# New prices for transfers and strided copies in a kernel that orders itself by a timing model

## The chip, the cores and the metric

The kernel runs on one core of a Trainium2 chip. The metric is the device time of one execution in microseconds; smaller is better. Three runs of the kernel before gave a median of 2499.2 us.

## The reference

A bidirectional encoder trunk of two layers over 272 tokens (16 meta tokens and 256 of the sequence), width 2048, in float32. Each layer has a mixer and a channel mixer:

```python
hn = rms_norm(h, mix_norm[layer])
c_q, c_kv, k_rope, u = split(hn @ w_in[layer])
att = mla_attention(c_q, c_kv, k_rope, ...)        # 8 heads, softmax over all 272 tokens
ssm = s5_mixer(u, ...)                             # complex diagonal scan, forward and backward, 64 groups
h = h + concat(rms_norm(att), rms_norm(ssm)) @ w_out[layer]
hn = rms_norm(h, ffn_norm[layer])
h = h + swiglu(hn, ...)                            # layer 0: dense, hidden width 5632
h = h + moe_swiglu(hn, ...)                        # layer 1: top 2 of 8 experts, hidden width 1408
```

At the end comes a last `rms_norm`, and the 16 meta tokens are dropped.

## The kernel before

**Stages.** In time order: mixer of layer 0 (to about 350 us with the first half of its output product), dense feed-forward, mixer of layer 1, experts. The weights come from DRAM in blocks of 512 KB through a ring of five `raw` buffers. In layer 0 the first 40 blocks are used as they are; after them ACT makes a rounded copy `wh` and DVE the rest `wl`, and each step of a product is three matmuls (`XH` by `wh`, `XL` by `wh`, `XH` by `wl`).

**The state-space part.** The columns u of the input product come first, in eight tiles. Each is scaled by DVE and stored to DRAM (`put_u`, L1433, into `uscr`); a pair of tiles is read back in another layout by two transfers (`load_u`, L959). `ssm_x` (L1037) multiplies four such groups by the tiles V, writes the products to PSUM, and copies them from there into the array X with strided access: on ACT in layer 0, on ACT and DVE in layer 1. In layer 0 the V tiles are made during this time from two transfers each (`pscr` and `ssm_bT`) by four DVE operations (`v_load`, `v_make`, L967 to L989); for layer 1 they are made during the dense part and stored. `ssm_scan` (L1083) then runs 66 steps of four DVE operations over X. After the attention `ssm_h` (L1101) copies pieces of X into the ring `rh`, and `ssm_y` (L1277) multiplies them, adds the Toeplitz part (made by `w_all`, L1125, and held in DRAM), copies the result into the ring `ry`, transposes it and applies GELU with a strided write. The first half of the output product, `w_out` (L1607), runs beside it: 16 column tiles of 8 steps.

**The order of the work.** Every engine runs its instructions in the order in which the program emits them. That order is found while the program is built: the parts above are generators, and `Sched.run` (L486) steps a main one (the products) and a list of side ones. A generator yields a condition or a time. A time is due when the modelled clock of PE has reached it (`ready`, L462); a name stands for "DVE's modelled clock is less than so far ahead of PE's". Where nothing is due, the modelled clock of PE is moved on by 100 ns.

**The model.** `Model` (L245) keeps a clock for each engine and, for each piece of memory, when it was last written and read. Costs of one instruction come from `pe_cost`, `dve_cost` (L426) and `act_cost` (L432); to the end of each the entry of its engine in `OUT` (L248) is added before its result counts as there. `Model.dma` (L348) takes 500 ns for an issue (600 on the Pool queue), 650 ns to the start, one nanosecond for 90 elements, and `OUT["DMA"]` to the landing. `rdy` (L634) asks the model when memory is ready and adds 200 ns; the generators that follow a transfer yield that time: X after `load_u`, the V products after `v_load`, the Toeplitz part after its loads, `ssm_y` after its loads, the transposes of the experts' tokens after the gather (`fetch`, L1952, and `feeder`, L2017). None of these numbers is in the program that runs: there the semaphores hold each instruction until its data are there.

**Memory.** `Arena` (L70) gives out pieces of one large tile, from the low end unless `top` is asked for. `room` asks whether pieces would fit; several generators yield until they do.

Of the kernel before, what the change touches and what calls it, by code (L numbers as in the profile page):

```python
# [24 lines left out]
NC = 68  # L25
TC = 4
# [43 lines left out]
class Arena:  # L70


    def __init__(self, t, n):
        self.t, self.n, self.live = t, n, []
        self.peak = 0
# [52 lines left out]


class Ring:  # L130
    def __init__(self, arena, n, shape, p=128):
        self.h = [arena.get(shape, p) for _ in range(n)]
        self.i = 0

    def next(self):
# [109 lines left out]
class Model:  # L245


    OUT = {"PE": 197.0, "DVE": 127.0, "ACT": 152.0, "DMA": 960.0}  # L248

    def __init__(self):  # L250
        self.t = {"PE": 0.0, "DVE": 0.0, "ACT": 0.0, "DGE": 0.0, "DMA": 0.0}
# [84 lines left out]
    def mark(self, eng, e, ins, outs):  # L336
        e += self.OUT[eng]
        for ap in ins:
            n, u = self.where(ap)
            if u is not None:  # L340
                r = self.mem[n][1]
                r[u] = np.maximum(r[u], e)
        for ap in outs:
            n, u = self.where(ap)
            if u is not None:
                self.mem[n][0][u] = e

    def dma(self, q, out, *ins):  # L348
        t = max(self.q.get(q, 0.0), self.ready(*ins))
        n, u = self.where(out)  # L350
        if u is not None:
            t = max(t, self.mem[n][0][u].max(), self.mem[n][1][u].max())
        t = max(t, self.t["DGE"]) if q != "pool" else t
        e = t + (500.0 if q != "pool" else 600.0)
        self.q[q] = e
        if q != "pool":
            self.t["DGE"] = e
        d = max(self.t["DMA"], e + 650.0) + size_all(out) / 90.0
        self.t["DMA"] = d
        self.mark("DMA", d, ins, [out])  # L360
        if self.log is not None:
            self.log.append(("DMA", d - size_all(out) / 90.0, d, "dma"))
        return d + 960.0


def size_all(ap):
    n = 1
    for x in ap.shape:
        n *= x
    return n  # L370


def size(ap):
    n = 1
    for x in ap.shape[1:]:
        n *= x
    return n
# [35 lines left out]
def psum(ap):  # L413
    return "PSUM" in str(ap.space)
# [10 lines left out]

def dve_cost(name, a, k):  # L426
    n = size(a[0]) if name != "tensor_reduce" else size(a[1])
    f = 65.0 + (63.0 if any(psum(x) for x in a) else 0.0)
    return f + n * {"reciprocal": 6.4, "memset": 0.3, "tensor_scalar": 0.6}.get(name, 1.05)


def act_cost(name, a, k):  # L432
    return (52.0 if psum(a[1]) else 93.0) + (93.0 if "accum_out" in k else 0.0) + 0.84 * size(a[0])


class Proxy:
    def __init__(self, nc, sched):
        self._nc = nc
        m = sched.m
        self.vector = Eng(nc.vector, m, "DVE", dve_cost)  # L440
        self.scalar = Eng(nc.scalar, m, "ACT", act_cost)
        self.tensor = Eng(nc.tensor, m, "PE", pe_cost)
        self.sync = Eng(nc.sync, m, "SP", None)
        self.gpsimd = Eng(nc.gpsimd, m, "pool", None)
# [87 lines left out]
class Kern:  # L532
# [568 lines left out]
    def ssm_h(self, l, F):  # L1101

        nc, st = self.nc, self.st
        yield self.has("scan", l)
        yield self.has("att", l)
        yield lambda: F.room(2 * 4 * 2 * NC)
        X = st["X"]
        rh = st["rh"] = Ring(F, 2, [4, 2, NC])
        st["hq"], st["hn"], n = [], 0, 0
        for t in rh.h:  # L1110
            nc.vector.memset(t.ap, 0.0)
        for T in TORD:
            for a in (0, 4):
                yield lambda: n - st["hn"] < 2
                t = rh.next()
                yield self.s.m.clear(t)
                g = 8 * T + a
                nc.scalar.activation(t[0:64, :, :, 1:NC],
                                     X[0:64, :, :, g:g + 4].rearrange("p s r g -> p g r s"), AF.Copy)
                nc.vector.tensor_copy(t[64:128, :, :, 0:NC - 1],  # L1120
                                      X[64:128, ::-1, :, g:g + 4].rearrange("p s r g -> p g r s"))
                st["hq"].append((t, self.rdy(t)))
                n += 1
# [153 lines left out]
    def ssm_y(self, l, F):  # L1277

        nc, st = self.nc, self.st
        q0 = NMETA if l else 0  # L1280
        N, k0 = L - q0, q0 // TC
        yield self.has("scan", l)
        yield lambda: "rh" in st and self.R is not None and F.room(8 * N, 512, 512) and self.R.room(8 * N, 8 * N)
        R = self.R
        g_ = st["g"] = F.get([8, N], top=True)
        gh, gl = st["gh"], st["gl"] = R.get([8, N]), R.get([8, N])
        ry = Ring(F, 2, [TC, 8, 16], NC)
        idn = self.cst[:NC, CI:CI + NC]

        def turn(T, y, t):  # L1290
            yield t
            bank = yield from self.grab()
            ps = bank[:, :L].rearrange("p (t k) -> p t k", t=TC)
            for j in range(TC):
                nc.tensor.transpose(ps[:, j], y[:, j].rearrange("p g c -> p (g c)"), idn)
            nc.scalar.activation(g_[:, T].rearrange("p (k t) -> p t k", t=TC), ps[:, :, k0:], AF.Gelu_apprx_tanh)
            self.drop(bank)
            nc.scalar.activation(gh[:, T], g_[:, T], AF.Copy)
            yield self.rdy(gh[:, T])
            nc.vector.tensor_tensor(gl[:, T], g_[:, T], gh[:, T].bitcast(F32), op=OP.subtract)  # L1300
            st["nT"] += 1

        st["nT"] = 0
        for i, T in enumerate(TORD):
            yield lambda: i in st["wq"]
            w, m, u, t = st["wq"].pop(i)
            yield t
            yield lambda: i - st["nT"] < 2
            y = ry.next()
            bank = yield from self.grab()  # L1310
            ps = bank[:NC].rearrange("p (g t c) -> p g t c", g=8, t=TC)
            for a in (0, 4):
                yield lambda: len(st["hq"]) > 0
                H, t = st["hq"].pop(0)
                yield t
                for g in range(4):
                    b = (a + g) // GW[l], (a + g) % GW[l]
                    for r in range(2):
                        nc.tensor.matmul(ps[:, a + g], H[:, g, r], w[:, b[0], r, :, b[1]], start=(r == 0), stop=False)
                    nc.tensor.matmul(ps[:, a + g], u[:, a + g, T // 4],  # L1320
                                     m[:, a + g].rearrange("p (t c) -> p t c", t=TC), start=False, stop=True)
                    if g % 2:
                        yield None
                st["hn"] += 1
            st["yn"] = i + 1
            nc.scalar.activation(y.rearrange("p t g c -> p g t c"), ps, AF.Copy)
            self.drop(bank)
            self.s.add(turn(T, y, self.rdy(y)))
        yield lambda: st["nT"] == 8
        for r in (ry, st["rh"], st["U"], st["X"]) + st["rw"]:  # L1330
            r.free()
        self.flags.add(("Y", l))
# [1058 lines left out]
```

## Time and profile before

| | |
|---|---|
| median of three runs | 2499.2 us |
| lowest and highest | 2496.71 and 2500.32 us |
| the profiled execution's own time | 2494.38 us |
| its span, first to last instruction | 2492.5 us |
| its mean granted PE clock | 0.985 |
| busy: PE, DVE, ACT, Pool | 97%, 77%, 55%, 6% |

The profile is of one execution, shorter than the median; sums made from its rows stand against its own time. Busy time of PE is modelled at its ends, so a high share does not say that every matmul ran at full rate; the idle time in front of an instruction and the granted clock of a window say where time was lost. Nearly all operations are recorded at L408, the line of the wrapper that feeds the model, and all ordinary DMA issues at L390; so groups are told apart by the names of what they write and read. `fa` and `ra` are the arenas, `bank` is PSUM. A matmul on plain float32 data shows as two records.

### The profile page before, as it was taken

What the parts mean: (1) busy time and instruction counts of PE and PEld (TensorE: products, weight loads), DVE (VectorE), ACT (ScalarE), POOL (GpSimd) and SP (SyncE); (2) the same over time, 40 slices, a digit from 0 to 9 for tenths busy, and PEclk for the clock granted to TensorE, in tenths of its full rate; (3) what the DMA queues carried; (4) which work ended last, traced back from release to release, by engine and by line L of the source; (5) the groups of instructions that cost most, each with busy time, mean ns of one, the idle gap of its engine ahead of it and who ended that gap; (6) DMA issues with size and microseconds to landing.
All of it is one profiled execution on the core that took longest, in us unless ns stands there. A gap on an engine that the chain in (4) does not pass through costs nothing. (4 is left out here: it accounts for less than half of the span.)

```text
span 2492.5 us, 42294 instructions
## 1 busy us (share of the span) xinstructions
PE 2427.1 (97%) x15930; PEld 2187.0 (88%) x15930; DVE 1920.4 (77%) x3282; ACT 1375.0 (55%) x1876; POOL 152.2 (6%) x262
## 2 busy tenths in 40 slices
PE   8899999999999999999999899999999999999997
PEld 6676699999999999999999759987888888888886
DVE  8788657787766666555666987668999999999997
ACT  4324566443333333334455456546777877877775
POOL 3400110011100000000011001000000000000000
PEclk9999899999999999999999989999999999999998
DMA  7842554568755555555566316657999999999995
GB/s 258 230 149 86 141 157 151 167 215 269 261 187 194 188 191 190 172 177 170 178 205 195 127 44 204 236 201 271 387 355 350 385 341 371 365 330 372 360 336 198
DMA packets 192919, 583.47 MB, mean 234 GB/s; under 512 B 36225, under 2 KB 48897, under 8 KB 191553
## 3 DMA queue, kind: packets, MB, share of 16 engines
q1 hardware_dynamic: 174802, 520.42, 60.0%
q0 software_dynamic: 17040, 57.97, 7.7%
q8 instruction: 127, 2.08, 0.3%
q10 hardware_dynamic: 864, 2.28, 0.3%
q14 instruction: 86, 0.70, 0.1%
HBM read 560.14 MB, written 22.54 MB: 234 GB/s over the span
## 5 line engine op out<-in xcount | busy, mean ns | idle before, releaser
L408 DVE TENSOR_TENSOR wl<-raw,wh 128x1024 fp32r<-128x1024 f32 (+1 forms) x559 | 667.6, 1202 | 194.2 <-ACT wh L408 188.4
L408 ACT ACTIVATE wh<-raw 128x1024 fp32r<-128x1024 f32 (+1 forms) x559 | 579.8, 1040 | 318.9 <-PE bank L408 231.4
L408 PE MATMUL bank<-XH,wh 128*128 128x272 f32 (+1 forms) x2160 | 636.8, 295 | 0.8 <-ACT tmpr L408 0.5
L408 PE MATMUL bank<-XH,wl 128*128 128x272 f32 (+1 forms) x2160 | 623.0, 288 | 3.1 <-DVE wl L408 3.1
L408 PE MATMUL bank<-XL,wh 128*128 128x272 f32 (+1 forms) x2160 | 620.8, 287 | 1.6 <-DVE XL L408 1.3
L408 PEld LDWEIGHTS bank<-XH,wh 128*128 128x128 f32 x2160 | 407.6, 189 | 5.1 <-ACT tmpr L408 0.7
L408 PEld LDWEIGHTS bank<-XH,wl 128*128 128x128 f32 x2160 | 407.1, 188 | 4.5 <-DVE wl L408 4.5
L408 PEld LDWEIGHTS bank<-XL,wh 128*128 128x128 f32 x2160 | 407.9, 189 | 2.6 <-DVE XL L408 2.2
L408 PE MATMUL bank<-ra,wh 128*128 128x272 f32 (+1 forms) x1792 | 341.1, 290 | 1.8 <-ACT wh L408 1.8
L408 PEld LDWEIGHTS bank<-ra,wh 128*128 128x128 f32 x1792 | 280.7, 188 | 6.5 <-issue 2.4
L408 PE MATMUL bank<-fa 128*68 128x64 f32 (+11 forms) x1892 | 263.5, 279 | 21.9 <-DMA fa<-uscr 10.2
L408 PEld LDWEIGHTS bank<-fa 128*68 128x68 f32 (+6 forms) x1892 | 196.1, 161 | 83.8 <-issue 50.4
L408 DVE TENSOR_TENSOR fa<-fa 128x128 f32<-128x128 f32 (+9 forms) x687 | 236.2, 353 | 43.0 <-ACT fa L408 16.9
L408 PE MATMUL bank<-ra,wl 128*128 128x272 f32 (+1 forms) x896 | 256.6, 286 | 0.8 <-DVE wl L408 0.8
L408 PE MATMUL bank<-wh,XH 128*128 128x512 f32 (+1 forms) x584 | 222.6, 381 | 0.7 <-ACT fa L408 0.4
L408 ACT ACTIVATE fa<-bank 64x268 f32<-64x268 f32 (+9 forms) x281 | 138.6, 500 | 150.4 <-PE bank L408 133.2
L408 PE MATMUL bank<-wh,XL 128*128 128x512 f32 (+1 forms) x584 | 220.1, 377 | 0.0
L408 PE MATMUL bank<-wl,XH 128*128 128x512 f32 (+1 forms) x584 | 219.0, 375 | 0.0
L408 PE MATMUL bank<-wh,ra 128*128 128x512 f32 x552 | 185.7, 393 | 2.0 <-ACT fa L408 2.0
L408 PE MATMUL bank<-fa,raw 128*128 128x272 f32 x608 | 162.4, 405 | 7.2 <-DMA raw<-w_mix 6.4
L408 PEld LDWEIGHTS bank<-ra,wl 128*128 128x128 f32 x896 | 168.6, 188 | 1.0 <-DVE wl L408 1.0
L408 DVE TENSOR_TENSOR wl<-h,wh 128x1024 fp32r<-128x1024 f32 (+1 forms) x137 | 157.0, 1156 | 9.9 <-ACT wh L408 7.4
(127 smaller groups left out, 3232.6 us busy)
## 6 DMA issues: line engine op xcount, KB each, us to landing
raw<-w_dense SPq DMA_DIRECT2D x264, 512.0 KB, 3.4
raw<-w_mix SPq DMA_DIRECT2D x150, 512.0 KB, 3.4
raw<-w_moe_g SPq DMA_DIRECT2D x106, 512.0 KB, 5.5
h<-w_moe_g SPq DMA_DIRECT2D x80, 512.0 KB, 5.8
raw<-w_moe_d SPq DMA_DIRECT2D x73, 512.0 KB, 6.7
h<-w_moe_d SPq DMA_DIRECT2D x59, 512.0 KB, 6.6
raw<-w_moe_t SPq DMA_DIRECT2D x51, 384.0 KB, 4.0
h<-w_moe_t SPq DMA_DIRECT2D x44, 384.0 KB, 4.1
```

What stands on the lines that cost most here:

```text
L408: return f(*a, **k)
```

## The change

The entry of `OUT` for transfers goes from 960 to 2260 ns, and so does the same number in what `Model.dma` returns. A new test `apart` finds operands of three or more dimensions whose last one is not contiguous. ACT copies with such an operand, and DVE copies from PSUM into such an operand, are priced 80 ns plus 2.05 ns an element. The rings `rh` and `ry` are taken from the upper end of their arena; `Ring` has a new argument for that. No instruction is added or taken out; their order and the addresses of the two rings, and of what is placed after them, can differ.

```diff
--- before.py
+++ after.py
@@ -128,8 +128,8 @@
 
 
 class Ring:
-    def __init__(self, arena, n, shape, p=128):
-        self.h = [arena.get(shape, p) for _ in range(n)]
+    def __init__(self, arena, n, shape, p=128, top=False):
+        self.h = [arena.get(shape, p, **({"top": True} if top else {})) for _ in range(n)]
         self.i = 0
 
     def next(self):
@@ -245,7 +245,7 @@
 class Model:
 
 
-    OUT = {"PE": 197.0, "DVE": 127.0, "ACT": 152.0, "DMA": 960.0}
+    OUT = {"PE": 197.0, "DVE": 127.0, "ACT": 152.0, "DMA": 2260.0}
 
     def __init__(self):
         self.t = {"PE": 0.0, "DVE": 0.0, "ACT": 0.0, "DGE": 0.0, "DMA": 0.0}
@@ -360,7 +360,7 @@
         self.mark("DMA", d, ins, [out])
         if self.log is not None:
             self.log.append(("DMA", d - size_all(out) / 90.0, d, "dma"))
-        return d + 960.0
+        return d + 2260.0
 
 
 def size_all(ap):
@@ -425,11 +425,20 @@
 
 def dve_cost(name, a, k):
     n = size(a[0]) if name != "tensor_reduce" else size(a[1])
+    if name == "tensor_copy" and psum(a[1]) and apart(a[0]):
+        return 80.0 + 2.05 * n
     f = 65.0 + (63.0 if any(psum(x) for x in a) else 0.0)
     return f + n * {"reciprocal": 6.4, "memset": 0.3, "tensor_scalar": 0.6}.get(name, 1.05)
 
 
+def apart(ap):
+
+    return ap.ap[-1][0] != 1 and len(ap.shape) > 2
+
+
 def act_cost(name, a, k):
+    if apart(a[0]) or apart(a[1]):
+        return 80.0 + 2.05 * size(a[0])
     return (52.0 if psum(a[1]) else 93.0) + (93.0 if "accum_out" in k else 0.0) + 0.84 * size(a[0])
 
 
@@ -1105,7 +1114,7 @@
         yield self.has("att", l)
         yield lambda: F.room(2 * 4 * 2 * NC)
         X = st["X"]
-        rh = st["rh"] = Ring(F, 2, [4, 2, NC])
+        rh = st["rh"] = Ring(F, 2, [4, 2, NC], top=True)
         st["hq"], st["hn"], n = [], 0, 0
         for t in rh.h:
             nc.vector.memset(t.ap, 0.0)
@@ -1284,7 +1293,7 @@
         R = self.R
         g_ = st["g"] = F.get([8, N], top=True)
         gh, gl = st["gh"], st["gl"] = R.get([8, N]), R.get([8, N])
-        ry = Ring(F, 2, [TC, 8, 16], NC)
+        ry = Ring(F, 2, [TC, 8, 16], NC, top=True)
         idn = self.cst[:NC, CI:CI + NC]
 
         def turn(T, y, t):
```

## Rows read from the trace of the kernel before

**Rows 1.** The page's head: span; busy time, share of span, instructions of PE.

```profile
span 2492.5 us, 42294 instructions
...
PE 2427.1 (97%) x15930; PEld 2187.0 (88%) x15930; DVE 1920.4 (77%) x3282; ACT 1375.0 (55%) x1876; POOL 152.2 (6%) x262
```

**Rows 2.** Windows by stage: busy us (instructions) of PE, PEld, DVE, ACT, POOL; granted clock, DMA.

```profile
350.00:1300.00 950.00, 947.24 (x7492) 935.92 (x7491) 635.06 (x973) 394.88 (x506) 42.95 (x80) 1.00 0.59 193
...
1350.00:1500.00 150.00, 138.24 (x828) 111.06 (x827) 132.12 (x401) 78.13 (x165) 6.88 (x11) 0.93 0.32 101
...
1735.00:2400.00 665.00, 665.00 (x3166) 568.25 (x3165) 618.98 (x638) 518.37 (x571) 3.76 (x4) 1.00 0.97 362
```

**Rows 3.** Waits of PE over the whole span: sum in us, times, longest.

```profile
PE bank L408 <- DMA fa<-uscr: 10.2, 5, 3.0
...
PE bank L408 <- DMA fa<-xtok,fa: 4.5, 2, 3.0
```

**Rows 4.** Time order on the Pool queue: start, us, instruction, idle before and its releaser.

```profile
58.87 0.56 POOL L390 DMA_DIRECT2D uscr<-fa  x1
...
64.63 0.70 POOL L390 DMA_DIRECT2D fa<-uscr  x1 [4.50 <-DMA uscr<-fa]
...
116.68 0.55 POOL L390 DMA_DIRECT2D uscr<-fa  x1 [2.23 <-DVE fa L408]
...
1304.48 0.55 POOL L390 DMA_DIRECT2D uscr<-fa  x1 [7.49 <-issue]
```

**Rows 5.** Time order on PE, mixers and start of the experts.

```profile
32.25 10.25 PE L408 MATMUL bank<-fa,raw 128*128 128x272 f32 x44
...
47.05 1.51 PE L408 MATMUL bank<-fa 128*128 128x136 f32 x12 [1.25 <-DMA fa<-uscr]
...
68.44 4.20 PE L408 MATMUL bank<-fa 128*128 128x136 f32 x20 [2.71 <-DMA fa<-uscr]
...
91.59 0.35 PE L408 MATMUL bank<-fa 128*64 128x96 f32 x2 [2.17 <-issue]
...
125.73 0.70 PE L408 MATMUL bank<-fa 128*128 128x136 f32 x4 [3.04 <-DMA fa<-uscr]
...
1311.60 1.25 PE L408 MATMUL bank<-fa 128*128 128x136 f32 x4 [2.57 <-DMA fa<-uscr]
...
1688.81 1.09 PE L408 MATMUL bank<-cst,fa 128*128 128x128 f32 x8 [3.00 <-DMA fa<-xtok,fa]
...
1713.26 0.66 PE L408 MATMUL bank<-cst,fa 128*128 128x128 f32 x4 [1.50 <-DMA fa<-xtok,fa]
```

**Rows 6.** Windows of five microseconds; the number behind POOL's is the granted clock.

```profile
70.00:75.00 5.00, 5.00 (x27) 4.43 (x26) 3.61 (x13) 3.83 (x8) 2.66 (x6) 0.78 0.65 161
...
125.00:130.00 5.00, 4.27 (x18) 3.88 (x19) 3.56 (x10) 3.17 (x6) 0.55 (x1) 0.68 0.73 228
...
280.00:285.00 5.00, 5.00 (x10) 1.88 (x9) 2.28 (x11) 1.93 (x7) 2.13 (x4) 0.50 0.26 63
...
1310.00:1315.00 5.00, 3.40 (x16) 3.44 (x17) 0.61 (x1) 1.16 (x2) 0.00 (x0) 0.66 0.42 141
1480.00:1485.00 5.00, 5.00 (x10) 2.46 (x10) 2.42 (x11) 1.29 (x4) 0.00 (x0) 0.50 0.01 3
```

**Rows 7.** DMA issues: KB each, median us from issue to landing.

```profile
fa<-uscr POOLq DMA_DIRECT2D x32, 136.0 KB, 5.1
```

**Rows 8.** Waits of DVE, 0 to 350 us.

```profile
DVE fa L408 <- DMA fa<-ssm_bT: 12.4, 5, 4.0
```

**Rows 9.** Groups by form: busy us, mean ns of one, idle before and releasers.

```profile
L408 ACT ACTIVATE fa<-bank 64x268 f32<-64x268 f32 x96 | 60.2, 635 | 31.3 <-PE bank L408 30.3
...
L408 PE MATMUL bank<-fa 128*128 128x136 f32 x256 | 43.5, 296 | 10.4 <-DMA fa<-uscr 10.2 <-issue 0.2
```

**Rows 10.** Windows of the second mixer, instructions that touch XH alone.

```profile
1497.00:1523.00 26.00, 25.17 (x141) 21.45 (x140) 0.48 (x1) 0.00 (x0) 1.00 0.81 254
1523.00:1565.00 42.00, 19.30 (x71) 12.70 (x70) 0.00 (x0) 0.00 (x0) 1.00 0.51 156
```

## The prediction

> **What bounds the kernel now.** Read the page's head first: TensorE (PE) is busy 97% of the span, so time can only be won where PE stands still or where its clock falls [rows 1]. Then the busy time by stage: the dense feed-forward part (350 to 1300 us) has 947 of 950 us busy at clock 1.00 and the steady part of the experts 665 of 665, so an order of emission can win nothing there; the second mixer's attention has 138 of 150 at clock 0.93 [rows 2]. The two mixers and the start of the experts are where the change can act. Third, the list of PE's waits: the largest sum is 10.2 us, in five waits for `fa<-uscr`, the transfers that bring the state-space input u back from DRAM; 4.5 us in two waits are for `fa<-xtok`, the gather of the experts' tokens [rows 3]. A wait here is not missing work: PE runs its instructions in the order of emission, and the matmul that stands next was emitted before its data could be there, while plain GEMM steps stood behind it in the queue. Fourth, the Pool queue and PE in order of time, to see what the model should have known [rows 4, 5]. Fifth, five-microsecond windows, since after each such stop the granted clock shows a stretch at the lower of its two levels, 1.2 instead of 2.4 GHz [rows 6].
>
> **The longer transfer, input u.** From the issue of a u tile's store to the first matmul on it the model adds: issue 0.60, start 0.65, 34,816 elements at 90 per ns 0.39, landing 0.96, margin 0.20 = 2.80 us for the store; two loads issued one after the other, 1.20 + 0.65 + 0.39 + 0.96 + 0.20 = 3.40. Sum 6.2 us. With 2.26 in the place of 0.96, twice, it is 8.8 us. The trace: store at 58.87, matmul at 68.44, 9.57 us; 116.68 to 125.73, 9.05 us; 1304.48 to 1311.60 in the second mixer, 7.12 us [rows 4, 5]. So the new price is nearly right in the first mixer and 1.7 us long in the second. Each of the five groups is emitted 2.6 us later, behind that much GEMM: in the first mixer those steps were going to run anyway, and a step is short against 2.6 us: 44 records at 32.25 take 10.25 us, two to a step, 0.47 us. The waits were 1.25, 2.71, 3.04 and 2.57 us, and by difference 0.6 for the fifth; 2.6 us off each leaves 0.11 and 0.44, and removes 9.6 of 10.2 us. The loads are moved on the Pool queue too, past the loads for the V tiles behind them, which now need not stand behind the 4.50 us for which the second load held the queue until its own store had landed [rows 4]; nothing else waits there. I take 8.0 us, because the model's clock and PE's differ by some tenths at each place. Ends: 0 (GEMM steps emitted ahead are themselves not ready) and 10.2.
>
> Here a page of the Trainium skill speaks against the change. "DMA: Bandwidth & Descriptors", section "Anatomy of one DMA", gives about 2.0 us plus the bytes at 436 GB/s, which for 136 KB is, as an estimate, 2.3 us: the old price, not the new. By it the five matmul groups would be held too long and the term above would be near nothing, as in the first rival below. The trace disagrees.
>
> These 32 loads have a median of 5.1 us from issue to landing [rows 7], and the sum goes by that.
>
> **The clock behind those stops.** Lost time is window times (1 - clock): 70 to 75 us 5 x 0.22 = 1.1; 125 to 130 us 1.6; 1310 to 1315 us 1.7 [rows 6]. Sum 4.4 us. If the stops shrink to 0.4 us or less, no fall should follow: the dense part has 2.8 us of pauses in it and a clock of 1.00 [rows 2]. I take 3.6 us; ends 0 and 4.4.
>
> **The longer transfer, V tiles.** VectorE (DVE) stood 12.4 us in five waits for `ssm_bT` [rows 8], with everything emitted behind it held. PE pays for one of them: the Toeplitz matmuls at 91.59 waited 2.17 us, and DVE had only just run the products in front of them. With the products 1.3 us later, other DVE work goes ahead and PE's stop shrinks by up to 1.3. I take 1.3 us, ends -1.3 (V is the input of the same X matmuls; it may come that much later) and 2.17. The Toeplitz tiles themselves go through DRAM in three transfers in a row, on SP and Pool, and come up to 3.9 us later; their first reader is Y, behind `w_out`'s steps. The loads of the next V are emitted only after the products, so they move back too; what covers that is the GEMM of the first mixer, and the scan behind X, which there has the whole attention before its result is wanted.
>
> **The gather of the experts' tokens.** At 1713.26 the transposes waited 1.50 us while the matmuls of expert 0 stood behind them: 1.3 us later they run first. 1.3 us won. The 3.00 us at 1688.81 stay: expert 0's own first half needs these rows, and nothing is left to go ahead [rows 5]. Ends 0 and 1.5.
>
> **Strided copies.** A 64x268 copy from PSUM takes 635 ns [rows 9]; the old price is 52 + 0.84 x 268 = 277 on ScalarE (ACT), the new one 80 + 2.05 x 268 = 629. 96 of them make 34 us that the model did not see. But the X matmuls in front of these copies stood idle 10.2 us for u, 0.2 us for issue and none for a copy to free their bank [rows 9]: a better price has no stop to take away there. The instructions themselves stay as they are. 0; ends -2 and +2 (three times one copy, either way).
>
> **The two rings.** `rh` and `ry` are as large as before and have the same writers and readers. At the arena's other end they lie on memory last used by other tiles, and the gap that they leave can let `ssm_y` start earlier or later. The cover is `w_out`, whose first half (128 steps of three matmuls) needs neither: in the second mixer two of three matmuls of a step show `XH`, so 141 + 71 records are 106 steps by 1565 us, when the last Y tile is turned, and 22 are left [rows 10]; at 26.0 us / 70 steps = 0.37 us that is 8 us by which Y may come late at no cost. 0; ends -3 (cover gone) and +2.
>
> **Sum.** 8.0 + 3.6 + 1.3 + 1.3 = 14.2 us won. All that is emitted after the first moved instruction is dealt anew, and new small stops must be expected; I set 3 us against it, two of the size at 47.05 (1.25) and one of 0.5. Net 11.2 us, from the profiled execution's 2494.4 (span 2492.5, 1.9 around it) to 2483.2. The median of the runs is 2499.2, 4.8 above the profiled one; so 2499.2 - 11.2 = 2488.0.
>
> **Rivals.**
> *The stops move, not go.* The GEMM that fills the u waits is missing later, or what waits for V waits at the same place as X. For it: after each quarter the V products come at their own pace, DVE's five waits. Against it: PE has GEMM without a break up to the attention. It would win the gather and a third of the rest: about 1.3 + 12.9 / 3 - 3 = 2.6 us, 2496.6.
>
> *The attention runs dry earlier.* At the end of both attentions no GEMM is left, and the clock lies at 0.50 for whole windows: the first row of two in the first mixer, of three in the second [rows 6]; a window there costs 2.5 us. If the scan and the Toeplitz work, delayed by longer transfers, lie deeper in the attention, each softmax step waits longer on DVE, PE stops one head earlier, and one more such stretch appears in each mixer: three windows, 7.5 us each and 15 for both, plus the 3 us of small stops. Against the 14.2 won that is 3.8 us slower, and with half of the gain lost as well 10.9: 2510. It decides from where two such stretches come, that is when PE in the last two heads stands still as long as at 1311.60 once more. Against it: the GEMM of the first mixer moves ahead and not away.
>
> *Tails better as well.* The same stretches can vanish by the new deal: two windows and three, 12.5 us at most; half of it gives 2488 - 6 = 2482, all of it 2475.
>
> *The change does not do what it says:* where the emission had nothing else to put in between, order and time stay: 2499. The steps of 0.47 us between the u groups speak against it.
>
> **How the numbers follow.** Chances: forecast 0.48, better tails 0.15, stops that move 0.14, no effect 0.06, attention dry 0.17. A measurement of this kernel tells about 0.2%, 5 us, from no change. Forecast and better tails lie below 2494: 0.63, less 0.01 of the forecast's spread that ends inside the band: faster 0.62. Same: the two middle cases and that 0.01, 0.21. Slower: 0.17. The range takes the better tails at 2474 and reaches to 2504, the middle of the attention rival's way from no change to 2510; about 2 in 10 lie outside. The likeliest case by itself lies between 2480 and 2495, by the ends of its terms.
>
> **What would show it.** Right: PE's list has `fa<-uscr` under 2 us; no clock below 0.9 in the windows after the first quarters of X; the Pool queue no longer stands over 3 us for a u store in the first mixer; one wait of about 3 us for the gather is left. Dense and expert stages as long as before. Wrong: waits of the same sum under the names of V, ACT or DVE; clock 0.50 for longer than two and three windows at the attentions' ends; Y in the second mixer ending more than 8 us behind the start of its gated units. A time above 2499 would put the cause in the attention and not in the transfers.

## The result and the profile after

The changed kernel takes 2478.08 us (median of 6 runs, 2471.20 to 2483.61) against 2496.45 us for the kernel before beside it (6 runs, 2493.45 to 2500.32): ratio 0.9924, 95% interval [0.9903, 0.9944]. It is faster by 18 us by the medians; 11 were forecast. The time that came lies 10 us under the forecast of 2488 and inside its range. Of these 10 us, 2.7 are the forecast's starting point: it took its sum from the median of three runs, 2499.2, and six runs have 2496.45.

The profiled execution of the changed kernel is the slowest of its six, 2483.61 us, 10.8 below the profiled one of before. The page's head, for [rows 1]:

```profile
span 2481.8 us, 42264 instructions
...
PE 2425.7 (98%) x15930; PEld 2186.6 (88%) x15930; DVE 1920.8 (77%) x3282; ACT 1373.5 (55%) x1876; POOL 151.1 (6%) x262
```

The windows by stage, for [rows 2]. Dense part and experts are as before to 0.3 us; the second mixer's attention, over the same times, has a lower clock than before (0.91 for 0.93).

```profile
350.00:1300.00 950.00, 946.98 (x7505) 935.92 (x7503) 634.04 (x970) 396.47 (x510) 44.22 (x82) 1.00 0.59 194
1350.00:1500.00 150.00, 138.75 (x816) 112.02 (x815) 133.10 (x405) 77.38 (x162) 5.54 (x9) 0.91 0.33 107
1735.00:2400.00 665.00, 665.00 (x3150) 566.22 (x3149) 619.06 (x637) 517.03 (x569) 3.76 (x4) 1.00 0.97 361
```

The waits of PE, for [rows 3] (sum, times, longest). The u waits fell from 10.2 to 2.3 us, the gather's from two to one. All waits in the list add up to 50.8 us before and 41.2 after; without these two names to 36.1 and 35.7.

```profile
PE bank L408 <- ACT fa L408: 6.7, 9, 2.0
PE bank L408 <- DVE fa L408: 4.7, 4, 1.9
...
PE bank L408 <- DMA fa<-xtok,fa: 3.2, 1, 3.2
PE bank L408 <- DMA fa<-uscr: 2.3, 3, 1.2
```

The Pool queue in order of time, for [rows 4]. In the first mixer the second load of a pair of u tiles is held 4.41, 0.53, 2.86 and 0.67 us for its store. The hold of 4.50 us at the second pair is gone, but the one of 4.41 us at the first pair is over the 3 us that the prediction's sign allowed; the X matmuls behind it (48.02, below) do not wait.

```profile
44.00 0.70 POOL L390 DMA_DIRECT2D fa<-uscr  x1 [4.41 <-DMA uscr<-fa]
...
57.26 0.56 POOL L390 DMA_DIRECT2D uscr<-fa  x1
...
63.42 0.69 POOL L390 DMA_DIRECT2D fa<-uscr  x1 [0.53 <-DMA uscr<-fa]
...
85.86 0.70 POOL L390 DMA_DIRECT2D fa<-uscr  x1 [2.86 <-DMA uscr<-fa]
...
109.35 0.70 POOL L390 DMA_DIRECT2D fa<-uscr  x1 [0.67 <-DMA uscr<-fa]
```

PE in order of time, for [rows 5]. The first group of X (48.02) and the last (115.59) do not wait, the second waits 1.23 us, two in the second mixer 0.80 and 0.23. The stop of 2.17 us at the Toeplitz matmuls is gone, and so is the second wait for the gather. New are two small stops in the last group of X, for ACT and for DVE. The three lines in the second block are the end of the state-space part in the second mixer, read below.

```profile
48.02 0.69 PE L408 MATMUL bank<-fa 128*128 128x136 f32 x4
...
68.84 0.70 PE L408 MATMUL bank<-fa 128*128 128x136 f32 x4 [1.23 <-DMA fa<-uscr]
...
115.59 0.63 PE L408 MATMUL bank<-fa 128*128 128x136 f32 x4
...
122.13 0.79 PE L408 MATMUL bank<-fa 128*128 128x136 f32 x4 [1.69 <-ACT fa L408]
...
128.49 1.59 PE L408 MATMUL bank<-fa 128*128 128x136 f32 x12 [1.90 <-DVE fa L408]
...
1305.26 1.63 PE L408 MATMUL bank<-fa 128*128 128x136 f32 x12 [0.80 <-DMA fa<-uscr]
...
1679.30 1.10 PE L408 MATMUL bank<-cst,fa 128*128 128x128 f32 x8 [3.16 <-DMA fa<-xtok,fa]
```

```profile
1557.06 0.36 PE L408 MATMUL bank<-XH,wh 128*128 128x256 f32 x1
...
1561.54 0.46 PE L408 MATMUL bank<-cst,fa 68*128 68x68 f32 x4 [0.68 <-ACT fa L408]
1561.81 0.48 PE L408 MATMUL bank<-ra,wh 128*128 128x256 f32 x2
```

Windows of five microseconds, for [rows 6]. Behind the groups of X the clock stays at its upper level, even where PE stood 1.90 us (125 to 130). At the end of the first attention it lies at or near the lower level from 265 to 285 us, longer than before.

```profile
70.00:75.00 5.00, 5.00 (x37) 4.44 (x37) 2.98 (x10) 4.85 (x9) 3.12 (x6) 1.00 0.99 275
...
125.00:130.00 5.00, 3.10 (x19) 2.25 (x18) 3.32 (x10) 0.51 (x1) 0.00 (x0) 1.00 0.12 40
...
265.00:270.00 5.00, 5.00 (x12) 1.69 (x11) 1.30 (x5) 1.36 (x5) 0.54 (x1) 0.50 0.28 70
...
280.00:285.00 5.00, 5.00 (x22) 3.22 (x22) 1.66 (x6) 1.38 (x4) 0.54 (x1) 0.53 0.28 66
...
1310.00:1315.00 5.00, 5.00 (x43) 5.00 (x42) 4.23 (x6) 2.44 (x4) 1.94 (x3) 1.00 0.86 294
```

The u loads land in 5.3 us (for [rows 7]) and DVE waits 6.3 us in four for `ssm_bT` (for [rows 8]):

```profile
fa<-uscr POOLq DMA_DIRECT2D x32, 136.0 KB, 5.3
```

```profile
DVE fa L408 <- DMA fa<-ssm_bT: 6.3, 4, 3.8
```

Two measures are used below. Each run comes with its span and the mean granted clock of PE: span x (1 - clock) is what the lower clock took (the *clock loss*), the span less that the *rest*. In the 58 runs of the kernel before that stood beside the experiments the clock went from 0.982 to 0.989, the clock loss from 27 to 45 us, and the span followed it, 0.84 us for each us of loss; the rest was 2458.3 us with a standard deviation of 2.3. So most of the spread between runs of one kernel is the clock, and the rest is the sharper measure of the stops. The profiles bear this out: in all thirteen, the rest less the sum of PE's waits lies between 2400.0 and 2406.3 us, though the waits themselves go from 33.8 to 59.4. A difference in the rest is a difference in PE's waits, to some 2 us.

### The profile page after: what moved, and what is told of

Read it like the earlier page. It is cut to its first block, busy times and chain, and to the rows that moved or that the text cites. A ratio compares the mean times of both kernels' runs of the same rounds, so it can differ in the third digit from the quotient of the medians.

```text
span 2481.8 us, 42264 instructions
## 1 busy us (share of the span) xinstructions
PE 2425.7 (98%) x15930; PEld 2186.6 (88%) x15930; DVE 1920.8 (77%) x3282; ACT 1373.5 (55%) x1876; POOL 151.1 (6%) x262
## 5 line engine op out<-in xcount | busy, mean ns | idle before, releaser
L408 PE MATMUL bank<-fa 128*68 128x64 f32 (+10 forms) x1892 | 261.3, 278 | 13.4 <-DVE XL L408 3.8
L408 PEld LDWEIGHTS bank<-fa 128*68 128x68 f32 (+5 forms) x1892 | 193.8, 160 | 75.4 <-issue 42.0
```

The lines of the kernel that those rows point to most:

```text
L408: return f(*a, **k)
```

## The experiments

All stand against runs of the kernel before on the same chip, in three groups, in which that kernel has medians of 2496.1, 2496.3 and 2492.2 us. The changed kernel has six runs in a group of its own; so kernels of different groups are best compared by ratio. R is the rest, C the clock loss, both in us and as means over the kernel's runs; the standard error of such a mean is 0.5 to 1.4 us for R and 1.0 to 2.5 for C (0.3 and 0.6 for the kernel before).

| kernel | median us | ratio, 95% interval | R | C |
|---|---|---|---|---|
| before (58 runs) | 2495.5 | 1 | 2458.3 | 35.8 |
| changed | 2478.1 | 0.9924 [0.9903, 0.9944] | 2442.3 | 33.8 |
| transfers and rings, old copies | 2479.3 | 0.9930 [0.9908, 0.9952] | 2449.2 | 28.1 |
| rings alone | 2494.9 | 0.9991 [0.9972, 1.0010] | 2457.9 | 34.5 |
| copies and rings | 2493.3 | 0.9989 [0.9973, 1.0006] | 2454.4 | 37.8 |
| changed, 2260 for u alone | 2480.5 | 0.9941 [0.9918, 0.9964] | 2445.9 | 33.9 |
| changed, 2260 for all but u | 2490.0 | 0.9974 [0.9956, 0.9992] | 2450.9 | 37.3 |
| changed, 1610 | 2481.4 | 0.9947 [0.9930, 0.9965] | 2449.7 | 30.4 |
| changed, 2910 | 2468.2 | 0.9885 [0.9861, 0.9910] | 2434.8 | 31.1 |
| changed, 3560 | 2471.1 | 0.9915 [0.9889, 0.9941] | 2439.2 | 33.0 |
| 2910, old copies | 2482.7 | 0.9947 [0.9927, 0.9968] | 2446.0 | 32.6 |
| 2910 for u, 2260 else | 2476.5 | 0.9934 [0.9914, 0.9954] | 2441.6 | 34.7 |
| 2260 for u, 2910 else | 2473.7 | 0.9921 [0.9902, 0.9940] | 2442.4 | 30.1 |

The theory: the transfers of input u were priced too short, and the gain is their waits and the clock behind them. The rivals: the strided copies or the rings carry it; the V tiles and the gather do.

**Transfers and rings, copies priced as before.**

```diff
 def apart(ap):
+    return False
...
```

> Both transfer prices (2260 for 960) and the two rings as in the changed kernel, the prices of copies as before. Theory, the transfers carry the gain: faster by 0.5 to 0.9%, 2476 to 2486 us against 2496, waits for `fa<-uscr` under 3 us in sum and none over 1.3 us. Rival, the strided copies carry it: within 0.2% of the kernel before, about 2496 us, though the u waits are gone. Rival, it takes both: half the gain, about 2488 us.

Measured: 0.9930 [0.9908, 0.9952], the changed kernel's time; u waits 1.4 us in two, the longest 1.1. The copies are not needed for the gain. But the two kernels get there differently: R is 6.9 us higher than in the changed kernel, C 5.7 lower. The longer price was not tried without the rings' new place.

**The rings alone.**

```diff
-    OUT = {"PE": 197.0, "DVE": 127.0, "ACT": 152.0, "DMA": 2260.0}
+    OUT = {"PE": 197.0, "DVE": 127.0, "ACT": 152.0, "DMA": 960.0}
...
-        return d + 2260.0
+        return d + 960.0
...
 def apart(ap):
+    return False
```

> Only the two rings at the arena's other end, both sets of prices as before. Theory (the rings are worth nothing by themselves): 2492 to 2500 us against 2496, the u waits at 10 us and the gather at 4.5 us as before. Rival, the rings give memory back earlier and so carry a part of the gain: 2486 to 2491 us, the attention of either mixer beginning over 3 us earlier with the u waits still there.

Measured: no change, 0.9991 [0.9972, 1.0010]; R as before. The theory holds for the time; in the profile the u waits are 12.6 us in six and the gather's 3.7, where 10 and 4.5 were expected. This run showed something else. From 255 us to a stop of 1.2 us near the end of its first attention, and through it, its PE does the same as in the kernel before, to 0.07 us. PE of before, then of the rings alone (start, us, instruction, idle before):

```profile
273.67 0.69 PE L408 MATMUL bank<-cst,fa 96*128 96x96 f32 x6
275.58 0.41 PE L408 MATMUL bank<-cst,fa 96*16 96x96 f32 x3 [1.21 <-DVE XL L408]
275.82 6.83 PE L408 MATMUL bank<-fa 128*96 128x272 f32 x19
```

```profile
273.61 0.69 PE L408 MATMUL bank<-cst,fa 96*128 96x96 f32 x6
275.52 0.40 PE L408 MATMUL bank<-cst,fa 96*16 96x96 f32 x3 [1.22 <-DVE XL L408]
275.76 6.31 PE L408 MATMUL bank<-fa 128*96 128x272 f32 x26
```

Then the clock of before falls, to 0.70 and, in the next window, to the 0.50 of [rows 6]; that of the other does not (windows, before first):

```profile
275.00:280.00 5.00, 4.42 (x18) 2.67 (x19) 3.62 (x14) 1.08 (x4) 0.00 (x0) 0.70 0.35 82
```

```profile
275.00:280.00 5.00, 4.48 (x23) 2.27 (x23) 4.14 (x16) 1.24 (x5) 0.00 (x0) 1.00 0.34 82
280.00:285.00 5.00, 4.71 (x34) 3.17 (x33) 4.25 (x19) 4.09 (x13) 2.46 (x4) 1.00 0.74 185
```

So the low clock at the end of an attention is not fixed by the order: one profile with it and one without are no evidence on a change. The Trainium skill, "TensorE: Matmul & The Clock Gate", section "Part 1: The HAM clock gate", gives a reason, which it states of the clock's rise at the start of a kernel: the stretches in which the chip judges activity run on freely and do not begin with the kernel, so runs of one kernel differ. These two profiles agree with it (0.50 in one, 1.00 in the other, behind the same stop); no run here shows where the stretches lie.

**Copies and rings, the old transfer price.**

```diff
-    OUT = {"PE": 197.0, "DVE": 127.0, "ACT": 152.0, "DMA": 2260.0}
+    OUT = {"PE": 197.0, "DVE": 127.0, "ACT": 152.0, "DMA": 960.0}
...
-        return d + 2260.0
+        return d + 960.0
```

> The changed kernel with the old transfer price (960): rings and copy prices alone. Theory: within 0.2%, 2492 to 2500 us against 2496, u waits near 10 us, attentions beginning within 2 us of where they began before. Rival, the copies carry the gain: 2478 to 2486 us. Rival, longer copies by themselves reorder for the worse: 2500 to 2505 us.

Measured: 0.9989 [0.9973, 1.0006], no difference that the runs can tell; the u waits are all there, one of 6.0 us:

```profile
PE bank L408 <- DMA fa<-uscr: 11.8, 5, 6.0
```

The theory holds for the time. Missed: the attentions begin 2.1 us earlier and 3.4 later than before, where at most 2 were expected. R is 3.5 us lower than with the rings alone, C 3.3 higher.

**The longer price for input u alone.**

```diff
+        far = any("uscr" in x.tensor.name for x in (out, *ins))
+        lag = self.OUT["DMA"] if far else 960.0
-        self.mark("DMA", d, ins, [out])
+        self.mark("DMA", d + lag - self.OUT["DMA"], ins, [out])
...
-        return d + 2260.0
+        return d + lag
```

> The changed kernel with the longer transfer price kept only for transfers that write or read the scratch of the input u (40 of them in each mixer); all others are priced at 960 again. Theory, the u waits and the clock falls behind them are most of the gain (8.0 + 3.6 of 14.2 us in the prediction): 2481 to 2488 us, `fa<-uscr` under 3 us, the gather's 1.5 us wait back, the start of the second mixer's attention some 10 us earlier than before. Rival, the gain is in the V tiles and the other transfers: 2491 to 2497 us with the u waits gone all the same. Rival, it all comes from u: 2476 to 2480 us.

Measured: 2480.5 us, 0.9941 [0.9918, 0.9964]: most of the gain, as the theory had it, and this price moves the kernel with copies and rings by 12.7 us (2493.3 to 2480.5): R by -8.5, C by -3.9. The u waits are nearly gone:

```profile
PE bank L410 <- DMA fa<-uscr: 1.0, 2, 0.8
```

The gather has 2.6 us in two waits, less than before. Missed: the second mixer's attention begins 13.9 us earlier than before (1416.54 against 1430.46, ScalarE's table load), not 10. The first attention begins later, 208.18 against 207.07, and yet this kernel is 9.2 us ahead at the end of the dense part (first store of u in the second mixer at 1287.24 against 1296.45). So the start of the attention does not tell how much GEMM was done ahead of it.

**The longer price for all but input u.** The same edit with `not far` in the place of `far`.

> The complement of the run with the longer price for input u alone: rings and copy prices as in the changed kernel, 2260 for every transfer but those that write or read the scratch of u, which keep 960. Theory, the terms add up: 2493.3 (rings and copies alone) less the 2.5 us by which the changed kernel stands below the run with u alone, 2488 to 2493 us, with the u waits still 8 to 12 us in sum. Rival, V tiles and gather carry a good half and u's part was shared with them: 2482 to 2487 us. Rival, u late beside everything else on time makes new stops: 2495 to 2502 us.

Measured: 2490.0 us, 0.9974 [0.9956, 0.9992], the theory's range. Ratios times 2495.5 give -2.7 us for copies and rings, -14.7 with the price for u, -6.5 with that for the rest; the two steps of -12.0 and -3.7 on top of -2.7 make -18.4, and the changed kernel has -19.0. The terms add up, though each of these figures has an interval of some 4 to 6 us either way. R says it more sharply: 2454.4 with neither price long, 2445.9 with u's, 2450.9 with the others', 2442.3 with both, so that u's price is worth 8.5 and 8.6 us and the others' 3.5 and 3.6, whichever comes first. The u waits came out a little under the 8 to 12 us: where X now stands, the loads for the V tiles are last nearly as often:

```profile
PE bank L410 <- DMA fa<-pscr: 8.5, 3, 3.5
...
PE bank L410 <- DMA fa<-uscr: 7.1, 4, 2.3
```

**Half of the step, and more than the step.** Three kernels, each with one number in both places:

```diff
-    OUT = {"PE": 197.0, "DVE": 127.0, "ACT": 152.0, "DMA": 2260.0}
+    OUT = {"PE": 197.0, "DVE": 127.0, "ACT": 152.0, "DMA": 1610.0}
...
-        return d + 2260.0
+        return d + 1610.0
```

> The changed kernel with a landing of 1610 ns, half of the step from 960 to 2260. Theory, a u group waits by what its two transfers are priced too short: 1.3 us less each, of 1.25, 2.71, 0.6, 3.04 and 2.57 us stay 0, 1.4, 0, 1.7 and 1.3, 4.4 us in sum, and the clock falls behind the three that stay: 2483 to 2489 us. Rival, any price over a small threshold does it: 2476 to 2481 us with u waits under 2.5 us. Rival, half the step does nothing: 2491 to 2496 us.

Measured at 1610: u waits of 4.3 us, for 4.4 expected, but 2481.4 us (0.9947 [0.9930, 0.9965]) for 2483 to 2489:

```profile
PE bank L408 <- DMA fa<-uscr: 4.3, 3, 1.6
```

The sum of the waits came out, their places did not: one of 1.1 us in the first mixer and two of 1.6 in the second, where 1.4 and 1.7 were put in the first and 1.3 in the second. So the close agreement is in part luck. The clock did not follow the waits in this profile: behind all three it stayed at 1.00. R has 4.7 of the 12.1 us that lie between 960 and 2260, somewhat under half, for half of the step; C is lower than in either, and the time is 2 us under the theory's range.

> The changed kernel with a landing of 2910 ns, a further half step. Store to matmul is then modelled as 10.1 us, 0.5 to 1.0 over the 9.1 to 9.6 of the trace. Theory, nothing is left to win in the u waits: 2475 to 2482 us, u waits under 1.5 us. Rival, a price over the true one holds work back and the attention runs dry earlier: 2483 to 2492 us, first attention ending over 4 us later than in the changed kernel. Rival, the margin helps further: under 2474 us.

> The changed kernel with a landing of 3560 ns, as far over 2260 as 960 lay under it: 11.4 us are modelled from store to matmul. Theory: u waits under 1 us as before, but X now lies 2.6 us later than it could in each group, which costs only where GEMM is missing: 2476 to 2484 us. Rival, too long is as bad as too short: 2490 to 2500 us. Rival, the longer the better: under 2474 us.

Measured at 2910: 2468.2 us, 0.9885 [0.9861, 0.9910], which only the last rival had; at 3560: 2471.1, 0.9915 [0.9889, 0.9941]. Input u has one wait of 0.5 us in the first and none in the second. The version with 2910 is the fastest that ran, 10 us below the changed kernel by the medians, though their intervals overlap a little. PE's waits add up to 33.8 us for 41.2, and no single name has most of the 7.4 between them. Its attentions begin at 190.38 and 1402.65 us (196.53 and 1417.67 in the changed kernel, before 207.07 and 1430.46). Holding X back beyond the true time cost nothing here; the likely reason is that the GEMM that takes its place was going to run anyway.

**Where the further 10 us of 2910 lie.** Three more kernels: 2910 with `apart` returning False, 2910 for u and 2260 for the rest, and the reverse. The edit of the second:

```diff
+        far = any("uscr" in x.tensor.name for x in (out, *ins))
+        lag = 2910.0 if far else 2260.0
-        self.mark("DMA", d, ins, [out])
+        self.mark("DMA", d + lag - self.OUT["DMA"], ins, [out])
...
-        return d + 2260.0
+        return d + lag
```

> Landing 2910 and the two rings, but the prices of copies as before. Theory, the copies' prices are worth nothing by themselves: within 4 us of the run with 2910 and the new prices (2468), 2464 to 2473 us. Rival, they pay once the transfers are priced long enough: 2475 to 2483 us, with waits of PE for ScalarE or VectorE over 4 us more in sum. Rival, 2468 was a lucky order: anything near 2478.

> The changed kernel with 2910 for the transfers of input u alone, 2260 for all others. Theory, the further gain of 2910 (10 us) is in u as the first one was: 2466 to 2473 us. Rival, it is in V tiles, constants and gather: 2475 to 2480 us, like the changed kernel. Rival, the sum needs both: about 2473, and the complement (2260 for u, 2910 for the rest) as much.

> The complement: 2260 for the transfers of input u, 2910 for all others. Theory, the further gain is in u: 2475 to 2480 us, within 0.2% of the changed kernel. Rival, it is in the other transfers: 2466 to 2472 us. Rival, the order by itself scatters by some us whatever price is moved: then neither this run nor the one with 2910 for u alone lies at 2468 or at 2478, and the two do not add up.

Measured: 2482.7, 2476.5 and 2473.7 us, in a group where the kernel before has 2492.2; the ratios are 0.9947, 0.9934 and 0.9921. The theory falls: 2910 for u alone gives nothing beyond the changed kernel (0.9924) that can be measured, nor does 2910 for the rest alone, and together they give ten (R 2441.6, 2442.4 and 2434.8, for 2442.3). And with 2910 the copies' prices are worth 14 us by the medians and 15 by the ratios, where at 960 they were worth nothing. Two rivals are left. Either the step needs both prices; or, as the last rival of the third has it, from 2260 on any new price deals a new order, and the orders lie some 5 us around each other (eight kernels with 2260 or more for u: 0.9885 to 0.9947, R from 2434.8 to 2449.2). These runs do not decide between them. For the old copies at 2910 the mark of their rival is there: PE waits more than with the new copies in four rows, by 1.6, 1.9, 1.4 and 1.8 us. With the old copies first, then with the new ones:

```profile
PE bank L408 <- DVE XL L408: 9.7, 8, 1.9
...
PE bank L408 <- ACT fa L408: 6.2, 9, 2.0
PE bank L408 <- DVE wl L408: 4.4, 6, 1.7
...
PE bank L408 <- DVE fa L408: 4.0, 5, 1.2
```

```profile
PE bank L408 <- DVE XL L408: 8.1, 8, 1.9
...
PE bank L408 <- ACT fa L408: 4.8, 6, 2.0
...
PE bank L408 <- DVE wl L408: 2.5, 4, 0.8
PE bank L408 <- DVE fa L408: 2.2, 2, 1.2
```

That is 6.7 of the 11.2 us by which R differs. Whether these stops come from the copies' prices or from one order among many stays open: no single price was found that carries the step from 2260 to 2910.

## Why the prediction was right, and where its sizes were off

**Direction and cause were right.** The gain is the price of the transfers, mostly of input u, and neither the rings nor (at either 960 or 2260) the copies change the time by what can be measured. Dense part and experts did not move. Of the medians 18 us were won where 11.2 were forecast. Of the two profiles it was 10.7 us of span, and that this is so near is luck: R fell by 13.0 us from one to the other and the clock loss rose by 2.3, where 7.6 and 3.6 won were forecast.

**Input u, 8.0 us.** The list of waits went down by 7.9; R by 8.5 when the price for u alone was lengthened. The arithmetic of the model's times (6.2 us priced, 9.1 to 9.6 in the trace) carried this. By itself it would have taken away 9.6 us; 8.0 was put by judgement, so that the last tenth is luck. The page of the Trainium skill that spoke against it, "DMA: Bandwidth & Descriptors", section "Anatomy of one DMA", would have had 2.3 us for such a load, by estimate, and nothing to win. The changed kernel's loads again take 5.3 us, so the measurement decides against it for this queue under this load.

**The clock, 3.6 us.** C is 3.9 us lower by the price for u alone and 3.5 where the other transfers are long too, each with a standard error near 2.7; over all, the changed kernel's C is 2.0 lower than before, which is within the noise.

The profiles show where the clock was won and where it was lost. By windows of five microseconds around the groups of X (35 to 150 and 1285 to 1375 us), the four profiles with 960 for u lose 3.4 to 8.5 us, 6.8 in that of before, and the nine with more lose 0 to 1.7. From 1375 to 1600 us, with the second attention, the three kernels with 960 for every transfer lose 10.2 us each, the nine with 2260 or more for some lose 11.9 to 15.4, and the one at 1610 loses 6.8. That looks like the rival of the attention that runs dry, in part and in the second mixer alone. It rests on one profile of each kernel, and what makes it was not tried. At the end of the first attention there is no such order: 0 to 12.0 us, with short and long prices alike, and the run with the rings alone has none where before has 6.8, behind the same instructions. So the prediction's sign of being wrong, a clock of 0.50 for longer at the attentions' ends, came (6.9 us more in the changed kernel's profile than in that of before), and half of it says nothing.

Two readings behind this term were too simple. A fall did not come after each stop: the waits of 1.25 and 0.58 us had none. And the dense part's clock of 1.00 is rounded: in the profile of before it holds a window at 0.66 (460 to 465 us) behind a stop of 1.34 us, and the changed kernel has the same stop (451.71) with no fall. So it was no evidence that small pauses are safe.

**V tiles and gather, 1.3 us each.** Their sum came out: from the kernel with u alone to the changed one R falls by 3.6 us and the median by 2.5, where 2.6 were forecast. Only the first half is borne out. PE's waits in front of the Toeplitz matmuls of the first mixer add up to 2.5 to 7.9 us in the four profiles with 960 for these transfers, to 1.9 at 1610, and to 0 to 1.2 in the eight with 2260 or more. DVE's waits for `ssm_bT` halved, but copies and rings at the old transfer price had them at 6.5 us already. The gather's term failed: its waits are 1.6 to 4.5 us in the four profiles with 960 for it and 3.1 to 4.8 in the eight with 2260 or more, and all but the changed kernel among those eight have two of them. That the changed kernel has one was the luck of its order.

**Small stops, 3 us against.** This term failed. The new stops are there (1.69 and 1.90 us in the last group of X), but the order before had as many of its own, which went: the waits under all other names are 36.1 us before and 35.7 after. A new deal replaces old small stops by new ones; charging only the new ones cost the sum 3 us.

**Strided copies, 0.** Right for the time at 2260, not for the stops. "A better price has no stop to take away there" looked at the X matmuls alone; R is lower with the new prices by 3.5, 6.9 and 11.2 us at 960, 2260 and 2910, and the profiles' waits by 7.2, 3.1 and 9.9. In the first two C is higher by 3.3 and 5.7 us (one and two standard errors), so the time shows none of it. Why the clock gives it back there and not at 2910 is open.

**The rings, 0.** Right: with the rings alone the time and R stay. But the cover that the prediction counted on, some 8 us of `w_out`, was used up in the changed kernel. There the last step of `w_out`'s first half starts at 1557.06 us; Y's last transposes follow at 1561.54, behind a stop of 0.68 us for ACT, and the gated units at once (1561.81). It cost no more than that. It is not the rings that did it: with the rings alone `w_out`'s first half still runs for 9.0 us behind Y's last transposes, as it does before, and with copies and rings, at 960, it ends 17.1 us ahead of them.

Over the runs, R fell by 16.0 us where 8.0 + 1.3 + 1.3 - 3 = 7.6 were forecast: copies and rings brought 3.9, u 8.5, the other transfers 3.6, and the 3 did not come. C fell by 2.0 for 3.6. So 6.8 us more were won than forecast by these means (7.2 by the medians), and the 2.7 us of the starting point are the rest of the miss. The right sign of the forecast rests on u; its size was low mostly because copies and rings were put at nothing, where R has 3.9 us, and new small stops at 3 us, which did not come.

## What to carry to other kernels

Where a kernel takes its order from a model, set the time that the model gives for a chain (store, load, use) beside the trace, and count per place how much later the step would be emitted. Here the sum of the waits held (7.9 us for 8.0, 4.3 for 4.4), the places less so. Price transfers rather too long than too short while other work is there to fill in: half of the step still left waits of 4.3 us, twice the step left none for u and cost nothing. A price that deals the whole order anew can move the time by some 5 us for which no cause is found; read the span less the clock loss over several runs, do not take one order's 5 us for the worth of a price, and do not take a wait that went in one profile for a term that came true.

## What the runs showed of the hardware

The size of a stop alone did not decide whether the clock fell behind it. With the price for u alone PE waited 2.52 us at 50.69 with no fall, and 1.69 us at 68.61 with one; in the changed kernel 1.90 us had none. PE and its windows in that run:

```profile
50.69 0.84 PE L410 MATMUL bank<-fa 128*64 128x96 f32 x8 [2.52 <-DMA fa<-ssm_bz]
...
68.61 0.71 PE L410 MATMUL bank<-fa 128*64 128x96 f32 x6 [1.69 <-DVE fa L410]
```

```profile
50.00:55.00 5.00, 4.31 (x30) 3.91 (x31) 3.99 (x13) 2.58 (x5) 2.04 (x4) 1.00 0.45 143
...
70.00:75.00 5.00, 5.00 (x23) 3.98 (x22) 4.38 (x15) 1.43 (x3) 1.74 (x4) 0.68 0.83 226
```

And one order of instructions, run many times, loses 27 to 45 us to the lower clock: as much as the whole change is worth lies between two runs of the same kernel.
